# Low halves last in each pair of k tiles, the norm vector in a load of its own, the state-space parameter work behind the first weight chunk

## The chip, the cores and the metric

One core of a Trainium2 chip. The metric is the device time of one execution in us; before the change three runs gave 888.95, 889.18 and 889.61 us, median 889.18.

## The reference

A decoder trunk of two layers and a final norm on 256 tokens of 2048 channels, in float32. Cut to what matters here:

```python
# even layer: state-space mixer and spatial gating side by side
h = rmsnorm(x, norm_g); proj = h @ w_in
xa, ga, zb, gb = split(proj)
ya = gelu(s5_mixer(xa, ...)); ya = ya * sigmoid(ya @ w_glu + b_glu) * silu(ga)
u, v = split(gelu(zb)); v = layernorm(v)
yb = u * (causal(w_sp) mixed over 128 positions of v + b_sp) * silu(gb)
x = x + concat([ya, yb]) @ w_out
# odd layer: differential attention, 8 heads of two maps
q, k, v, g = split(rmsnorm(x, norm_g) @ w_in); q, k = partial_rope(q), partial_rope(k)
a = softmax(q1 @ k1.T) - lam * softmax(q2 @ k2.T)        # causal
o = rmsnorm(a @ v, subln_g) * (1 - lambda_init) * silu(g)
x = x + o @ w_out
return rmsnorm(x)
```

`s5_mixer` first works out its parameters from `lam`, `log_dt`, `B` and `C` (exponentials, sines, products of 64 states), then runs the recurrence.

## The kernel before, in words

All large products are made of **chunks** of the weights: `stream` lists 140 chunks of 1 MB, each 512 input rows (4 k tiles of 128) by 512 output columns. Chunks 0 to 7 are v, 8 to 15 xa, 16 to 23 u, 24 to 31 gb, 32 to 39 ga, 40 to 47 and 52 to 59 the first output projection (eo, ep) with the gate's weights between, 60 to 123 layer 1 (for each of four pairs of heads q, k, v, g, four chunks each), 124 to 139 the last output projection od. `fetch` (L139) loads chunks on SyncE's queue three ahead, `split` (L156) divides each into two halves b0 and b1 of two k tiles, and makes of each half two tiles of 32-bit reduced format: `wh`, the weight rounded, a copy on ScalarE (`act`, L82), and `wl`, the exact rest, a subtraction on VectorE (`sub`, L61). There are three buffers each for `wh` and `wl`, so a new half can be made when TensorE has done with one three halves back, or with any that has come free. Activations are divided likewise (`hh` and `hl` in layer 0, `oh` and `ol` ahead of od). A product takes three matmuls for each weight tile: hi·wh, hi·wl, lo·wh; `gemm_t` (L201, 512 columns a matmul, 24 a chunk) puts tokens on the partitions and `gemm_c` (L213, 256 columns, 48 a chunk) channels. c17_1 means half b1 of chunk 17, and wh17_1 its rounded tile.

Beside this runs side work: the parameters of the state-space mixer (`ssm_params` L359, `e_tables`, `ssm_consts`), its recurrence, and attention. These are Python generators in the queue `side`; `run_side(n)` takes n steps of them at a place in the source. `run_side(5)` stands ahead of the loop over v, `run_side(2)` behind each chunk of v. A scheduler then orders the instructions of TensorE, VectorE, ScalarE and GpSimd by readiness and priority (the halves of weights at a high one), so that the order on an engine isn't that of the source. SyncE's queue keeps the source's order. Each engine works its instructions through in the built order.

The parameters arrive as one packed tensor `pkt` of 82 KB, the first load of all (L259); its first 16 columns `g0` are the norm's weights, which `h_split` needs for the first `hh` and `hl`. The parameter work begins with an exponential of a part of `pkt` (tiles e_x, e_n, e_r, e_p on VectorE). Later its results go over ScalarE into `bbr` and `cA` (from the products m1fc, m2fc, m1fa, m2fa, m1ab, m2ab) and by 64 small matmuls into `pk0`; `pbt` are transposes of `bbr`, `U2` copies of the mixer's input, `vscr` a sum of squares for the layer norm of v, `vt` that norm's result, `ut` the evacuation of u.

In layer 1 each head h of a pair p has this chain: `sc{p}{h}` scores on TensorE, softmax, `aT{p}{h}` transposes, `ah`/`al`, `o{p}{h}` (nine matmuls), a norm (two sums of squares on ScalarE, twelve operations `rq_` and two scalings on VectorE), a product with the gate, `oT{p}{h}` transposes, `oh`/`ol`. The output projection takes its chunks in the order n = 0 and 1 with k = 0, 1, 2, then (0, 3) and (1, 3), that is c130 and c131: k tiles 12 to 15 are the last pair's output, and half b1 (tiles 14 and 15) is its second head's. od0 and od1 hold both banks of the PSUM pool for these products until then.

Of the kernel before, what the change touches and what calls it, by code (L numbers as in the profile page):

```python
# [17 lines left out]
T = 256  # L18
# [11 lines left out]
def hybrid_trunk_kernel(ctx: ExitStack, tc: tile.TileContext, xT, xtok, w_in0, w_glu, w_out0,  # L30
# [53 lines left out]
    def rsqrt_mean(name, ss, n, eps, post=None):  # L84
        """(ss / n + eps) ** -0.5: an integer first guess, a cubic step and a Newton step."""
# [32 lines left out]
    # ---------------------------------------------------------------- weight stream  # L118
# [20 lines left out]
    def fetch(upto):  # L139
        while pos["f"] <= min(upto, len(stream) - 1):  # L140
# [5 lines left out]
            for a in range(0, 4, step):  # L146
                if i < 4:
                    xs = slice(4 * i + a, 4 * i + a + step)
                    SP.dma_start(out=xt[:, xs, :], in_=xT[:, xs, :])
                SP.dma_start(out=t[:, a:a + step], in_=src[:, a:a + step])  # L150
# [5 lines left out]
    def split(upto, before=None):  # L156
        """hi = the weight rounded to float32r, lo = the exact rest."""
# [43 lines left out]
    def gemm_t(ps, acts, ktiles, first, last):  # L201
        ws = next_chunk()
        for a, k in enumerate(ktiles):
            hi, lo = acts(k)
            wh, wl = ws[a]
            for t in range(2):
                s = slice(t * 128, (t + 1) * 128)
                PE.matmul(ps[:, t, :], hi[:, s], wh, start=first and a == 0, stop=False)  # L208
                PE.matmul(ps[:, t, :], hi[:, s], wl, start=False, stop=False)  # L209
                PE.matmul(ps[:, t, :], lo[:, s], wh, start=False,  # L210
                          stop=last and a == len(ktiles) - 1)

    def gemm_c(ps, acts, ktiles, first, last):  # L213
        ws = next_chunk()
        for a, k in enumerate(ktiles):
            hi, lo = acts(k)
            wh, wl = ws[a]
            for c in range(4):
                s = slice(c * 128, (c + 1) * 128)
                fin = last and a == len(ktiles) - 1  # L220
                PE.matmul(ps[:, c, :], wh[:, s], hi, start=first and a == 0 and c % 2 == 0, stop=False,  # L221
                          skip_group_check=True)
                PE.matmul(ps[:, c, :], wh[:, s], lo, start=False, stop=False, skip_group_check=True)  # L223
                PE.matmul(ps[:, c, :], wl[:, s], hi, start=False, stop=fin, skip_group_check=True)  # L224
# [13 lines left out]
    # ---------------------------------------------------------------- start: x^T, norm  # L238
# [20 lines left out]
    SP.dma_start(out=pkt, in_=pk)  # L259
# [10 lines left out]
    g0 = pkt[:, 0:16]  # L270
# [854 lines left out]
```

## Time and profile before

| | |
|---|---|
| median of three runs | 889.18 us (888.95 to 889.61) |
| span of the profiled execution | 887.3 us |
| TensorE busy | 871.7 us, 98% |
| VectorE busy | 666.3 us, 75% |
| ScalarE busy | 448.8 us, 51% |
| GpSimd busy | 38.3 us, 4% |
| loaded and stored | 160.24 MB, mean 181 GB/s |

The profile is of one execution; its span runs from the first to the last instruction, and no other time of that execution is recorded. A share of busy time is an average over stages of different kinds, so the waits of TensorE stage by stage say more than the shares.

### The profile page before, as it was taken

The page shows a single profiled execution, that of the slowest core. Times are in us where ns is not written, and L with a number is a line of the kernel's source. Part 1 is how long each engine was busy: PE and PEld are TensorE (multiplying, and loading weights), DVE is VectorE, ACT ScalarE, POOL GpSimd, SP SyncE. Part 2 cuts the span into 40 slices and gives each one's busy share as a digit, 9 for nine tenths or more (in the row PEclk, how much of TensorE's full clock was granted, in tenths as well). Part 3 has the DMA queues.
Part 4 walks back from the last instruction along what each step waited for, and adds up shares of the span by engine and source line. Part 5 has one row for each costly group of instructions (what it writes and reads, how often), then busy time and mean ns, then how long its engine had stood idle before and what let it go on. Part 6 is the DMA issues. An engine that isn't in the chain of part 4 may idle for free.

```text
span 887.3 us, 14016 instructions
## 1 busy us (share of the span) xinstructions
PE 871.7 (98%) x5598; PEld 778.4 (88%) x5598; DVE 666.3 (75%) x1219; ACT 448.8 (51%) x623; POOL 38.3 (4%) x47
## 2 busy tenths in 40 slices
PE   9999999999999999999999999999999999999995
PEld 7799978788999789889988999889988998888895
DVE  8999869999988866567866677666767577665773
ACT  6563862455334645565345543554346544554551
POOL 7110000000000100000000000000000000000000
PEclk9999999999999999999999999999999999999998
DMA  8965452234534655455554545554454455555542
GB/s 306 379 243 191 143 190 96 96 120 166 190 114 141 259 185 176 170 195 202 180 182 160 188 145 190 191 190 152 181 190 171 165 188 196 183 189 190 178 155 96
DMA packets 25985, 160.24 MB, mean 181 GB/s; under 512 B 2880, under 2 KB 4160, under 8 KB 7744
## 3 DMA queue, kind: packets, MB, share of 16 engines
q1 hardware_dynamic: 25344, 156.20, 49.2%
q0 software_dynamic: 576, 3.15, 1.0%
q8 instruction: 44, 0.72, 0.3%
q14 instruction: 21, 0.17, 0.1%
HBM read 157.24 MB, written 2.10 MB: 180 GB/s over the span
## 4 chain that ended last, share of the span: by engine, by line
PE 90%; DVE 7%; ACT 1%; issue 1%; DMA 0%; DVEq 0%; ACTq 0%
PE v L209 5%; PE v L210 5%; PE v L208 5%; PE k L224 3%; PE q L221 3%; PE k L223 3%; PE k L221 3%; PE q L224 3%; PE q L223 3%; PE g L210 3%; PE g L209 3%; PE g L208 3%; PE od L209 2%; PE od L208 2%; PE od L210 2%; PE ga L221 2%
## 5 line engine op out<-in xcount | busy, mean ns | idle before, releaser
L82 ACT ACTIVATE wh<-wr 128x1024 fp32r<-128x1024 f32 (+1 forms) x276 | 288.7, 1047 | 356.0 <-PE v L210 64.0
L61 DVE TENSOR_TENSOR wl<-wr,wh 128x1024 fp32r<-128x1024 f32 (+1 forms) x276 | 331.8, 1205 | 142.2 <-ACT wh L82 141.4
L224 PE MATMUL k<-h2h,wl 128*128 128x256 f32 x256 | 72.8, 284 | 0.0
L221 PE MATMUL q<-h2h,wh 128*128 128x256 f32 x256 | 72.7, 284 | 0.0
L223 PE MATMUL q<-h2l,wh 128*128 128x256 f32 x256 | 72.7, 284 | 0.0
L224 PE MATMUL q<-h2h,wl 128*128 128x256 f32 x256 | 72.6, 284 | 0.0
L221 PE MATMUL k<-h2h,wh 128*128 128x256 f32 x256 | 72.4, 283 | 0.0
L223 PE MATMUL k<-h2l,wh 128*128 128x256 f32 x256 | 72.4, 283 | 0.0
L209 PE MATMUL v<-wl,h2h 128*128 128x512 f32 x128 | 50.8, 397 | 0.0
L209 PE MATMUL g<-wl,h2h 128*128 128x512 f32 x128 | 50.3, 393 | 0.0
L210 PE MATMUL g<-wh,h2l 128*128 128x512 f32 x128 | 50.1, 391 | 0.0
L210 PE MATMUL v<-wh,h2l 128*128 128x512 f32 x128 | 50.0, 390 | 0.0
L208 PE MATMUL v<-wh,h2h 128*128 128x512 f32 x128 | 50.0, 390 | 0.0
L208 PE MATMUL g<-wh,h2h 128*128 128x512 f32 x128 | 49.9, 390 | 0.0
L224 PEld LDWEIGHTS k<-h2h,wl 128*128 128x128 f32 x256 | 49.1, 192 | 0.1
L221 PEld LDWEIGHTS q<-h2h,wh 128*128 128x128 f32 x256 | 49.1, 192 | 0.2
L221 PEld LDWEIGHTS k<-h2h,wh 128*128 128x128 f32 x256 | 49.1, 192 | 0.0
L223 PEld LDWEIGHTS k<-h2l,wh 128*128 128x128 f32 x256 | 49.1, 192 | 0.0
L223 PEld LDWEIGHTS q<-h2l,wh 128*128 128x128 f32 x256 | 49.1, 192 | 0.0
L224 PEld LDWEIGHTS q<-h2h,wl 128*128 128x128 f32 x256 | 49.1, 192 | 0.0
L209 PE MATMUL od<-wl,oh 128*128 128x512 f32 x96 | 37.6, 392 | 0.0
L208 PE MATMUL od<-wh,oh 128*128 128x512 f32 x96 | 37.5, 391 | 0.0
(331 smaller groups left out, 2182.8 us busy)
## 6 DMA issues: line engine op xcount, KB each, us to landing
wr<-in_w_in_dram SPq DMA_DIRECT2D x100, 1024.0 KB, 4.8
wr<-in_w_out_dram SPq DMA_DIRECT2D x32, 1024.0 KB, 4.8
wr<-in_w_glu_dram SPq DMA_DIRECT2D x4, 1024.0 KB, 4.7
wr<-in_w_in_dram SPq DMA_DIRECT2D x8, 256.0 KB, 4.5
wr<-in_w_in_dram SPq DMA_DIRECT2D x4, 512.0 KB, 7.9
xk<-in_xtok_dram SPq DMA_DIRECT2D x2, 1024.0 KB, 10.9
xr<-in_xtok_dram POOLq DMA_DIRECT2D x2, 1024.0 KB, 7.6
out_dram<-x SPq DMA_DIRECT2D x6, 256.0 KB, 2.6
```

Source lines behind the costliest of these rows:

```text
L61: (eng or V).tensor_tensor(out=o, in0=a, in1=b, op=op)
L82: A.activation(out=o, in_=i, func=f, **kw)
L208: PE.matmul(ps[:, t, :], hi[:, s], wh, start=first and a == 0, stop=False)
L209: PE.matmul(ps[:, t, :], hi[:, s], wl, start=False, stop=False)
L210: PE.matmul(ps[:, t, :], lo[:, s], wh, start=False, stop=last and a == len(ktiles) - 1)
L221: PE.matmul(ps[:, c, :], wh[:, s], hi, start=first and a == 0 and c % 2 == 0, stop=False, skip_group_check=True)
L223: PE.matmul(ps[:, c, :], wh[:, s], lo, start=False, stop=False, skip_group_check=True)
L224: PE.matmul(ps[:, c, :], wl[:, s], hi, start=False, stop=fin, skip_group_check=True)
```

## The change

Three edits. **The loads:** `g0` becomes a tile of its own, loaded first (8 KB), and the whole `pkt` is loaded behind the second k tile's piece of chunk 0, sixth instead of first on SyncE's queue. **The matmuls:** in `gemm_t` and `gemm_c` all matmuls with the high half of two k tiles come first (hi·wh, lo·wh), then those with the low half (hi·wl); for chunk 0 this goes tile by tile. Their number is the same. **The side work:** `run_side(5)` ahead of the loop over v goes, and 7 steps instead of 2 are taken behind chunk 0. Comments that the diff removes are left out.

```diff
@@ fetch
             for a in range(0, 4, step):
+                if i == 0 and a == 2:
+                    SP.dma_start(out=pkt, in_=pk)
@@ gemm_t
+        i = pos["i"]
         ws = next_chunk()
-        for a, k in enumerate(ktiles):
-            hi, lo = acts(k)
-            wh, wl = ws[a]
-            for t in range(2):
-                s = slice(t * 128, (t + 1) * 128)
-                PE.matmul(ps[:, t, :], hi[:, s], wh, start=first and a == 0, stop=False)
-                PE.matmul(ps[:, t, :], hi[:, s], wl, start=False, stop=False)
-                PE.matmul(ps[:, t, :], lo[:, s], wh, start=False,
-                          stop=last and a == len(ktiles) - 1)
+        step = 1 if i == 0 else 2
+        for a0 in range(0, len(ktiles), step):
+            pair = range(a0, a0 + step)
+            for a in pair:
+                hi, lo = acts(ktiles[a])
+                for t in range(2):
+                    s = slice(t * 128, (t + 1) * 128)
+                    PE.matmul(ps[:, t, :], hi[:, s], ws[a][0], start=first and a == 0, stop=False)
+                    PE.matmul(ps[:, t, :], lo[:, s], ws[a][0], start=False, stop=False)
+            for a in pair:
+                hi, lo = acts(ktiles[a])
+                for t in range(2):
+                    s = slice(t * 128, (t + 1) * 128)
+                    PE.matmul(ps[:, t, :], hi[:, s], ws[a][1], start=False, stop=last and a == len(ktiles) - 1)
@@ gemm_c (likewise, always in pairs: 16 matmuls with wh, then 8 with wl)
...
@@ start
-    SP.dma_start(out=pkt, in_=pk)
+    g0 = const.tile([128, 16], F32, name="g0")
+    SP.dma_start(out=g0, in_=pk[:, 0:16])
...
-    g0 = pkt[:, 0:16]
@@ layer 0: v
-    run_side(5)
...
-            run_side(2)
+            run_side(7 if n == 0 and k == 0 else 2)
```

With this the scheduler's order changes in many places, also far from the edits. Three of them follow, in the order in which the engine gets its instructions; a name's last number tells buffers apart.

VectorE at the start, before (e_x to e_p are the exponential; hl0 and wl0_0 the low parts that the first matmuls need):

```order
L76 TENSOR_SCALAR e_x_215<-pkt_81 128x32
L61 TENSOR_TENSOR lprod_4116<-pkt_81 128x2
L74 TENSOR_SCALAR e_n_217<-e_x_215 128x32
L74 TENSOR_SCALAR e_n_217<-e_n_217 128x32 x2
L79 SCALAR_TENSOR_TENSOR e_r_221<-e_n_217,e_x_215 128x32
L79 SCALAR_TENSOR_TENSOR hl0_154<-xt_82,pkt_81,hh0_152 128x256
L79 SCALAR_TENSOR_TENSOR e_r_221<-e_n_217,e_r_221 128x32
L74 TENSOR_SCALAR e_p_224<-e_r_221 128x32
L74 TENSOR_SCALAR e_n1_233<-e_n_217 128x32
L79 SCALAR_TENSOR_TENSOR e_p_224<-e_p_224,e_r_221 128x32
L61 TENSOR_TENSOR wl0_0_157<-wr0_89,wh0_0_156 128x512
```

and now:

```order
L79 SCALAR_TENSOR_TENSOR hl0_156<-xt_82,g0_88,hh0_154 128x256
L61 TENSOR_TENSOR wl0_0_159<-wr0_90,wh0_0_158 128x512
L79 SCALAR_TENSOR_TENSOR hl0_156<-xt_82,g0_88,hh0_154 128x256
L76 TENSOR_SCALAR e_x_262<-pkt_81 128x32
L61 TENSOR_TENSOR lprod_4118<-pkt_81 128x2
L61 TENSOR_TENSOR wl0_0_159<-wr0_90,wh0_0_158 128x512
L74 TENSOR_SCALAR e_n_264<-e_x_262 128x32
```

The first hl0 and wl0_0 stand ahead of the exponential, and e_x now stands between the low halves of the first two k tiles.

ScalarE around chunks 16 and 17, where u begins, before:

```order
L82 ACTIVATE bbr1_648<-m2fc_659 64x32x16 x2
L82 ACTIVATE wh16_0_1653<-wr16_1535 128x1024
L82 ACTIVATE bbr0_646<-m1fa_702 64x32x16 x2
L82 ACTIVATE bbr1_648<-m2fa_703 64x32x16 x2
L82 ACTIVATE vscr0_934,vss_933<-vt_212,mu_930 128x1024
L82 ACTIVATE vscr1_961,vss_960<-vt_212,mu_957 128x1024
L82 ACTIVATE wh16_1_1657<-wr16_1535 128x1024
L82 ACTIVATE cA_650<-m1ab_714 64x32x16 x2
L82 ACTIVATE wh17_0_2021<-wr17_1593 128x1024
L82 ACTIVATE cA_650<-m2ab_715 64x32x16 x2
L82 ACTIVATE U2_208<-xs0_1267 32x512 x8
L82 ACTIVATE wh17_1_2025<-wr17_1593 128x1024
```

and now:

```order
L82 ACTIVATE wh16_1_1659<-wr16_1537 128x1024
L82 ACTIVATE wh17_0_2023<-wr17_1595 128x1024
L82 ACTIVATE bbr1_650<-m2fc_661 64x32x16 x2
L82 ACTIVATE bbr0_648<-m1fa_704 64x32x16 x2
L82 ACTIVATE bbr1_650<-m2fa_705 64x32x16 x2
L82 ACTIVATE vscr0_936,vss_935<-vt_214,mu_932 128x1024
L82 ACTIVATE vscr1_963,vss_962<-vt_214,mu_959 128x1024
L82 ACTIVATE cA_652<-m1ab_716 64x32x16 x2
L82 ACTIVATE cA_652<-m2ab_717 64x32x16 x2
L82 ACTIVATE U2_210<-xs0_1269 32x512 x8
L82 ACTIVATE vt_214<-vt_214,vnb_954,vrs_943 128x1024
L82 ACTIVATE wh17_1_2027<-wr17_1595 128x1024
```

wh17_0 has moved ahead of m2fc, m1fa, m2fa, vscr and the first cA, so that these, the second cA, U2 and one vt now lie between wh17_0 and wh17_1, where only the second cA and U2 lay.

TensorE in the last output projection, around the transposes of the last head (oT31), before (the rest of c128_1, all of c129 and the start of c130_0 stand between the nine matmuls of o31 and these rows):

```order
L208 MATMUL od0_7850<-wh130_0_8024,oh8_6842 128x512
L209 MATMUL od0_7850<-wl130_0_8025,oh8_6842 128x512
L210 MATMUL od0_7850<-wh130_0_8024,ol8_6843 128x512
L924 MATMUL oT31_7838<-ident_132,o231_7834 128x128 x4
L208 MATMUL od1_7953<-wh131_0_8058,oh8_6842 128x512
L209 MATMUL od1_7953<-wl131_0_8059,oh8_6842 128x512
```

and now, from the last three of o31's nine matmuls on (the first two stand ahead of c131_0's four low-half matmuls, the other seven behind them):

```order
L920 MATMUL o31_7804<-v_hi_4158,ah31_7800 128x256
L920 MATMUL o31_7804<-los_4159,ah31_7800 128x256
L920 MATMUL o31_7804<-v_hi_4158,al31_7801 128x256
L935 MATMUL oT31_7840<-ident_134,o231_7836 128x128 x4
L214 MATMUL od0_7852<-wh130_1_8030,oh8_6844 128x512
L214 MATMUL od1_7955<-wh131_1_8064,oh8_6844 128x512
L215 MATMUL od0_7852<-wh130_1_8030,ol8_6845 128x512
```

o31 has moved behind the high-half matmuls of c131_0, and oT31 follows its last matmul directly; the first product behind oT31 is c130_1, where it was c131_0.

## Rows read from the trace of the kernel before

**Rows 1.** The page: busy time, share of the span and instructions of TensorE (PE), its weight loads (PEld), VectorE (DVE), ScalarE (ACT), GpSimd (POOL).
```profile
PE 871.7 (98%) x5598; PEld 778.4 (88%) x5598; DVE 666.3 (75%) x1219; ACT 448.8 (51%) x623; POOL 38.3 (4%) x47
```

**Rows 2.** The windows view, one stretch of the span, within layer 1. Columns: the stretch in us and its length, busy us (and instructions) of PE, PEld, DVE, ACT, POOL, the granted clock of TensorE (1.00 is the upper of its two levels), the share of the DMA engines, GB/s.
```profile
420.00:780.00 360.00, 360.00 (x2340) 329.60 (x2340) 250.78 (x382) 175.81 (x250) 6.75 (x8) 1.00 0.51 179
```

**Rows 3.** The waits of TensorE: tile and line that waited, the engine and tile waited for, us in total, times, the longest.
```profile
PE v L209 <- DVE wl L61: 1.6, 2, 0.8
PE gb L208 <- ACT ut L82: 1.4, 1, 1.4
...
PE u L209 <- DVE wl L61: 0.8, 1, 0.8
PE pbt L521 <- ACT bT L82: 0.8, 1, 0.8
PE u L208 <- ACT ut L82: 0.5, 1, 0.5
PE eo L209 <- DVE wl L61: 0.4, 1, 0.4
```

**Rows 4.** The timeline of the start. Columns: start us, duration us, engine, line, operation, out<-in, shapes, and in brackets the idle time ahead of it and what ended it. hh and hl are the two parts of the activations; L208, L209 and L210 are the matmuls hi·wh, hi·wl and lo·wh.
```profile
3.53 0.51 ACT L82 ACTIVATE hh<-xt,pkt 128x256 fp32r<-128x256 f32 x1 [1.22 <-DMA xt<-in_xT_dram]
...
5.53 0.51 DVE L79 SCALAR_TENSOR_TENSOR hl<-xt,pkt,hh 128x256 fp32r<-128x256 f32 x1
...
5.85 0.80 PE L208 MATMUL v<-wh,hh 128*128 128x512 f32 x1
...
6.74 0.68 DVE L61 TENSOR_TENSOR wl<-wr,wh 128x512 fp32r<-128x512 f32 x1
...
7.47 0.80 PE L209 MATMUL v<-wl,hh 128*128 128x512 f32 x1 [0.82 <-DVE wl L61]
...
9.77 0.63 PE L208 MATMUL v<-wh,hh 128*128 128x512 f32 x1
...
10.20 0.53 PE L209 MATMUL v<-wl,hh 128*128 128x512 f32 x1
...
10.80 0.40 PE L208 MATMUL v<-wh,hh 128*128 128x512 f32 x1
...
11.03 0.39 PE L209 MATMUL v<-wl,hh 128*128 128x512 f32 x1
...
11.26 0.39 PE L210 MATMUL v<-wh,hl 128*128 128x512 f32 x1
```

**Rows 5.** The timeline of ScalarE from 92 to 116 us, where parameter work of the state-space mixer stands between the weight halves (same columns).
```profile
92.72 1.26 ACT L82 ACTIVATE bbr<-m2fc 64x512 f32<-64x512 f32 x2
...
96.93 1.27 ACT L82 ACTIVATE bbr<-m2fa 64x512 f32<-64x512 f32 x2
98.23 1.15 ACT L82 ACTIVATE vscr<-vt,mu 128x1024 f32<-128x1024 f32 x1
...
101.60 1.25 ACT L82 ACTIVATE cA<-m1ab 64x512 f32<-64x512 f32 x2
103.12 1.06 ACT L82 ACTIVATE wh<-wr 128x1024 fp32r<-128x1024 f32 x1 [0.26 <-PE xa L223]
...
105.36 5.30 ACT L82 ACTIVATE U<-xs 32x512 f32<-32x512 f32 x8
...
111.65 1.23 ACT L82 ACTIVATE vt<-vt,vnb,vrs 128x1024 f32<-128x1024 f32 x1
```

**Rows 6.** The timeline of TensorE about 97 to 99 us: the first and the last row of pk0's 64 small matmuls.
```profile
97.04 0.22 PE L506 MATMUL pk<-cN,bbr 128*32 128x32 f32 x1
...
99.03 0.23 PE L506 MATMUL pk<-cN,bbr 128*32 128x32 f32 x2
```

**Rows 7.** The timeline from 812 to 829 us, where the last head's attention ends: the last matmul of o31 (o), of its norm on VectorE the ninth of twelve operations, the scaling (o<-o,ro, two operations), the gate, the transposes oT31 (oT) and their two parts oh and ol. In between a low half of a weight (wl) on VectorE, behind the eighth of them, and two matmuls of the output projection (od) on TensorE.
```profile
814.97 0.28 PE L909 MATMUL o<-v_hi,al 128*128 128x256 f32 x1
...
817.77 1.23 DVE L61 TENSOR_TENSOR wl<-wr,wh 128x1024 fp32r<-128x1024 f32 x1
...
818.92 0.15 DVE L61 TENSOR_TENSOR rq_z<-ro 128x2 f32<-128x2 f32 x1
...
819.70 0.88 DVE L79 SCALAR_TENSOR_TENSOR o<-o,ro,l1c 128x256 f32<-128x256 f32 x2
...
821.64 0.68 DVE L61 TENSOR_TENSOR o<-o,gate 128x512 f32<-128x512 f32 x1
821.69 0.39 PE L210 MATMUL od<-wh,ol 128*128 128x512 f32 x1
...
824.41 0.39 PE L210 MATMUL od<-wh,ol 128*128 128x512 f32 x1
...
824.65 0.60 PE L924 MATMUL oT<-ident,o 128*128 128x128 f32 x4
...
825.81 0.58 ACT L82 ACTIVATE oh<-oT 128x512 fp32r<-128x512 f32 x1
...
827.08 0.68 DVE L61 TENSOR_TENSOR ol<-oT,oh 128x512 fp32r<-128x512 f32 x1
```

**Rows 8.** The timeline of TensorE at the program's end (two matmuls of 256 columns, the second its last), and the windows view of the last 6 us (columns as in rows 2).
```profile
873.83 0.28 PE L1016 MATMUL od3b<-hlast,oh 128*128 128x256 f32 x1
...
878.03 0.28 PE L1018 MATMUL od3b<-hlast,ol 128*128 128x256 f32 x1
...
881.00:887.30 6.30, 0.00 (x0) 0.00 (x0) 1.80 (x6) 0.72 (x1) 0.00 (x0) 0.50 0.44 166
```

More of the change, by code (lines that the diff above doesn't have):

```diff
@@ L213, in gemm_c @@
     def gemm_c(ps, acts, ktiles, first, last):
         ws = next_chunk()
[L215 to L224, printed above, removed]
+        cs = [(c, slice(c * 128, (c + 1) * 128)) for c in range(4)]
@@ new lines, in gemm_c @@
+        for a0 in range(0, len(ktiles), 2):
+            for a in (a0, a0 + 1):
+                hi, lo = acts(ktiles[a])
+                for c, s in cs:
+                    PE.matmul(ps[:, c, :], ws[a][0][:, s], hi, start=first and a == 0 and c % 2 == 0, stop=False,
+                              skip_group_check=True)
+                    PE.matmul(ps[:, c, :], ws[a][0][:, s], lo, start=False, stop=False, skip_group_check=True)
+            for a in (a0, a0 + 1):
+                hi, lo = acts(ktiles[a])
+                for c, s in cs:
+                    PE.matmul(ps[:, c, :], ws[a][1][:, s], hi, start=False, stop=last and a == len(ktiles) - 1,
+                              skip_group_check=True)
```

## Prediction

> **What bounds the kernel now.** I read the page first: TensorE is busy 98% of the span, VectorE 75, ScalarE 51 [rows 1]. So the time is TensorE's instructions plus TensorE's holes, and the views to read next are those that show holes. The windows say where to look: in 420 to 780 us TensorE is busy all of 360.00 us [rows 2], so nothing waits there. The list of TensorE's waits names the holes one by one: two of 0.8 us in v for the low half of a weight, 1.4 at gb for ut, 0.8 in u for a low half, 0.8 at pbt for bT, 0.5 in u for ut, 0.4 in eo for a low half [rows 3]. They add up to 5.5 us of 887.3. All sit in layer 0; layer 1, where two thirds of the time lies, has none. So this kernel offers a reordering little to win and, with TensorE full, much to lose: any new hole is paid in full.
>
> The profiled span is 887.3 us, the median of the runs 889.18, 1.9 us more, lying around the span. I work out differences inside the span and add them to 889.18. A measurement here can tell 0.2%, 1.8 us, from no change.
>
> **The matmuls themselves: 0.** The diff only permutes them. Every matmul loads its own weights before and after (as many weight loads as matmuls [rows 1]), and the three forms follow each other at the same 0.23 us once the clock is up [rows 4]. So putting the low-half matmuls last is free, and what counts is only who arrives when.
>
> **Start: -0.9.** The first matmul, on the high half, starts at 5.85, the next one at 7.47, because it needs the low half that VectorE began at 6.74 only, behind e_x, e_r and e_p [rows 4]. After the change hl·wh stands second; hl was written at 5.53 with its inputs there at 4.1, so nothing is waited for. The hole is 1.62 less one cold spacing of 0.43 (9.77 to 10.20), so 1.19 us. But these matmuls run at half speed until 10.20: if the clock rises at the same moment, 1.19 us hold 2.8 more cold matmuls, worth 2.8 x 0.23 = 0.64 later. If it rises as much earlier as the work does, all 1.19 is won. I take 0.9 between them; bounds 0 (e_x must now wait for the parameter load, which is issued behind four pieces, and VectorE's next low half queues behind e_x) and -1.2. The small first load only brings g0, and hh starts at 3.53 anyway when its piece of x arrives [rows 4], so it is worth nothing by itself.
>
> **Low halves later needed: -0.8 and -0.4.** The second v wait and the eo wait [rows 3] are for a low half wanted one matmul behind the first high one. Now eight matmuls, 1.8 us, come first, which is more than either wait. Bounds 0 and the full 1.2 together; I take the full.
>
> **The parameter work behind chunk 0: +4.2.** This is the first new hole. ScalarE's queue now has wh17_0 ahead of both m2fc operations, both a-sets, vscr, both cA, U2 and one vt, and wh17_1 behind all of them (the ScalarE order above). wh17_0 needs a buffer that TensorE frees with the last high-half matmul of c15_1; call that moment T. From T ScalarE needs 1.06 (wh) + 1.26 + 2 x 1.27 (bbr: m2fc, m1fa, m2fa, whose operations are of one shape) + 2 x 1.15 (vscr) + 2 x 1.25 (cA) + 5.30 (U) + 1.23 (vt) + 1.06 (wh17_1) = 17.2 us [rows 5]. TensorE has for that time: eight low-half matmuls at 0.12 (1.0), pk0 from 97.04 to 99.03 (2.1 [rows 6]) and pbt (1.0), and 36 matmuls of c16 and c17_0 at 0.227 (8.2), together 12.2. So 5.0 us are idle, in three pieces: pk0 for m2fc (1.06 + 1.26 - 0.96 = 1.4), pbt00, which needs pk0's bank read out, and c17_1 for the rest. Before, u lost 0.8 at this place [rows 3]. Net +4.2. Bounds: 0 if the operations of rows 5 find their turn as early as before, +6 if vscr's readouts and gaps between operations lengthen the queue by a tenth.
>
> **Waits that vanish behind it: -2.7.** TensorE comes about 2 us late to pbt's second half and both ut hand-overs (0.8, 0.5, 1.4 [rows 3]), and on ScalarE bT and ut now stand at most one operation further forward. I take all three as gone; bounds -2.7 and 0.
>
> By here the change stands at -0.9 - 0.8 - 0.4 + 4.2 - 2.7 = -0.6, about nothing.
>
> **The end of attention: +6.3.** This is the term that decides. In the output projection, half b1 of c130 and c131 needs the last head's output: o31, its norm, oT31, then oh and ol. Before, TensorE has the rest of c128_1, all of c129 and c130_0 between o31 and oT31: 42 matmuls, 9.7 us from 814.97 to 824.65, and the chain fits inside [rows 7]. After the change the scores of a pair are mostly put behind g, all of attention slides some 20 us, and the order above has nothing between o31 and oT31, with c130_1 right behind. The chain costs, from the start of the last o31 matmul: 2.80 to the end of eight of the twelve norm operations (814.97 to 817.77, two readouts on ScalarE ahead of them); 0.78 for four more (818.92 to 819.70); 0.80 for both o2; 0.68 for the gate. That is 5.06; the two low halves that stood within it are now ahead or behind. Then oT31 0.60, oh 0.58, ol 0.68 [rows 7], some 0.3 of hand-overs: 7.2. TensorE's own work in this time is the last o31 (0.1), four oT31 (0.4) and two high-half matmuls (0.45): 6.3 idle. Bounds 4.1 (the 5.06 alone less that work) and 7.2 (all of it).
>
> **The clock: +2.1.** At the end of the profile TensorE stops at 878.3, and from 881.0 on the granted clock is 0.50, its 1.2 GHz level [rows 8]: it fell within 2.7 us of the stop. The hole above holds 4.9 us without a matmul. So I expect the clock to fall in it, and c130_1 to start at the 0.43 spacing. At the start matmuls of v ran at that spacing from 5.85 to 10.20; the same 4.35 us here do the work of 2.3, so 2.1 are lost. Bounds: 0 (the clock stays), and 4.2 if the slow stretch lasts twice as long. The Trainium skill, "TensorE: Matmul & The Clock Gate", section "Part 1: The HAM clock gate (the "warmup" mystery)", says that the count of slow matmuls after a start varies from run to run of one kernel; no run so far shows that, and by it this term would be no constant, and the sum 895 to 897 from run to run.
>
> **Sum:** 889.18 - 0.6 + 6.3 + 2.1 = 896.98, so 897.0 us.
>
> **The rivals.**
> *The clock holds.* Four transposes and two matmuls interrupt the hole; if they keep the clock at its upper level only 6.3 is paid: 889.18 - 0.6 + 6.3 = 894.9. For it: the hole of 1.4 us before gb [rows 3] left the granted clock at 1.00. Against it: the fall at the end. Chance 0.28.
> *The spacing shrinks, so faster.* Place: all 84 chunks of 24 matmuls of 512 columns and 52 of 48 of 256, with od3 some 4700 matmuls. Putting two matmuls on the high half before one on the low half changes which operand follows which, and a spacing smaller by d ns gives 4.7 us per ns of d; from 1.3 ns on it wipes out 6.0 of the 7.8 and the time is within 0.2%, from 2.1 ns on it is faster: with 2.3 ns, 1% of 227, 897.0 - 10.8 = 886.2. For it: the spacing of 0.227 (12 steps from 821.69 to 824.41 [rows 7]) and 0.120 (35 steps from 873.83 to 878.03 [rows 8]) is above what 2.4 GHz would make of 512 and 256 columns, 0.213 and 0.107. Against it: two forms that share hi follow each other exactly as two that don't [rows 4]. The Trainium skill, "TensorE: Matmul & The Clock Gate", section "Wait — 56ns, not 53.3ns?", gives 215.7 ns for back-to-back matmuls of 512 columns; the trace differs, 227, and by the page's spacing the room for this rival would be 11 ns. Chance 0.08, and 0.03 that a milder form leaves the time the same.
> *The late attention collides everywhere.* Scores of all four pairs move behind g, into the next pair's q, where VectorE also works on q's rotation. If three boundaries each cost one low half, 1.2 us, and c132 another 0.5, the time is 897.0 + 4.1 = 901.1. Against: at each there are 4 to 10 us of matmuls between a score and its use. Chance 0.08.
>
> **How the numbers follow.** Forecast 897.0: 0.53. Its own range by the bounds that I think live (start, queue and clock each 1 us off): 895.5 to 899. The clock rival reaches down to 894.9, less 2.5 if the chain is at its lower bound or the queue fits better: 892.3. These two have 0.81, and 892 to 899.5 leaves little of them out. Slower by over 0.2% (above 891.0): 0.53 + 0.28 + 0.08 = 0.89. The same: 0.03. Faster (below 887.4): 0.08.
>
> **What would show it.** Right: the waits of TensorE list oT <- VectorE (the gated o2) with 4 to 5 us in one piece near 825, then od <- ScalarE or VectorE for oh and ol; the granted clock is 0.50 for some us right behind; matmuls of od at 0.43 spacing; u or pk waits of 1 to 3 us near 100 to 116, no v <- wl wait at 5.85 and 42, no gb <- ut. Wrong: no wait at oT above 1 us, matmuls of layer 1 closer than 0.227 and 0.120 (the second), a hole of 5 us with the clock at 1.00 throughout (the first), waits of about a microsecond at each q of layer 1 (the last), or in layer 0 a sum that differs from -0.6 by more than 2.

## The result, and the profile after

The changed kernel takes 901.1 us (median of four runs, 900.06 to 901.86) against 889.07 before: ratio 1.0131, 95% interval 1.0117 to 1.0145, slower by 12.0 us where 7.8 were forecast, and outside the range. The profiled execution took 900.49 us, 0.6 below the median; its span is 898.8 (before 887.3).

The busy line of the page after, which answers to [rows 1]:

```profile
PE 874.3 (97%) x5598; PEld 780.2 (87%) x5598; DVE 668.0 (74%) x1219; ACT 451.1 (50%) x623; POOL 37.8 (4%) x47
```

The work is the same. TensorE is busy 2.6 us longer, which goes with matmuls at the lower clock; the rest is holes. The waits of TensorE after (columns as in [rows 3]):

```profile
PE oT L935 <- DVE o L61: 5.1, 1, 5.1
PE u L214 <- DVE rq_i L74: 1.9, 1, 1.9
PE v L220 <- DVE wl L61: 1.6, 1, 1.6
PE pk L518 <- ACT bbr L82: 1.4, 1, 1.4
PE pbt L533 <- DVE intra L61: 1.2, 1, 1.2
...
PE od L214 <- ACT oh L82: 0.7, 1, 0.7
PE gb L214 <- ACT ut L82: 0.6, 1, 0.6
PE u L214 <- ACT ut L82: 0.5, 1, 0.5
```

Five waits of over a microsecond, where before only gb had one (psw's 1.1 at the very start, left out, is there in both). Those of oT, pk and pbt were forecast; v's was not, and u's was put at another place, at c17_1 instead of u's first matmul. A list of waits misses what a slow clock costs, so the table below uses another measure: for each matmul the time to the next one's start, less the median for its shape (227 ns for 512 columns, 120 for 256, 109 for 128, 25 for 32, the same before and after), added up by stretch of the span. Small negative sums come from pairs of unlike shapes; the differences between rows are what counts. E1 to E14 are the experiments below.

| us lost in | 0–20 | 20–80 | 80–120 | 120–180 | 180–420 | 420–820 | from 820 | sum |
|---|---|---|---|---|---|---|---|---|
| before | 5.5 | 1.1 | 1.1 | 3.5 | -3.5 | 1.3 | 0.1 | 8.9 |
| after | 4.6 | 2.0 | 6.2 | 1.9 | -3.4 | 0.1 | 8.7 | 20.2 |
| E1 old order from layer 1 on | 5.0 | 3.1 | 6.1 | 2.0 | -3.4 | 1.3 | 0.1 | 14.0 |
| E2 new order alone | 5.1 | 0.6 | 4.7 | 1.6 | -3.7 | 0.1 | 9.6 | 17.8 |
| E3 loads and side work | 5.8 | 1.6 | 6.1 | 3.4 | -4.5 | 1.4 | 0.1 | 13.9 |
| E4 loads, chunk 0 | 5.1 | 1.6 | 6.2 | 3.0 | -4.8 | 1.3 | 0.1 | 12.5 |
| E5 after, hole filled | 5.0 | 1.9 | 6.1 | 2.0 | -3.4 | 0.2 | 4.9 | 16.6 |
| E6 after, early clearings | 4.0 | 0.0 | 6.1 | 2.0 | -3.4 | 0.1 | 9.8 | 18.5 |
| E7 chunk 0 alone | 5.8 | 1.0 | 1.1 | 3.7 | -3.7 | 1.2 | 0.1 | 9.2 |
| E8 loads alone | 5.6 | 1.4 | 6.4 | 2.8 | -4.8 | 1.3 | 0.1 | 12.8 |
| E9 after, m2fc first | 4.3 | 1.9 | 6.9 | 1.6 | -3.4 | 0.2 | 8.8 | 20.2 |
| E10 three chunks | 5.6 | 0.5 | 0.4 | 2.4 | -3.1 | 1.2 | 0.1 | 7.1 |
| E11 three chunks, early clearings | 8.9 | 0.0 | 0.4 | 3.8 | -4.5 | 1.3 | 0.1 | 9.8 |
| E12 more VectorE work | 7.0 | 0.2 | 7.5 | 1.9 | -4.5 | 1.4 | 0.1 | 13.6 |
| E13 as E2, two low halves back | 4.4 | 0.6 | 2.4 | 1.8 | -3.0 | 0.1 | 9.5 | 15.8 |
| E14 after, two low halves back | 5.1 | 1.9 | 6.2 | 1.6 | -3.4 | 0.2 | 9.8 | 21.4 |

After less before, from the unrounded sums: -0.9, +0.9, +5.1, -1.5, +0.1, -1.1, +8.7; together 11.2 of the span's 11.5.

**The end of attention.** The timeline after from o31's last matmul on (columns as in [rows 4]; answers to [rows 7]):

```profile
829.76 0.28 PE L920 MATMUL o<-v_hi,al 128*128 128x256 f32 x1
...
833.40 0.88 DVE L79 SCALAR_TENSOR_TENSOR o<-o,ro,l1c 128x256 f32<-128x256 f32 x2
834.31 0.69 DVE L61 TENSOR_TENSOR o<-o,gate 128x512 f32<-128x512 f32 x1
835.15 1.09 PE L935 MATMUL oT<-ident,o 128*128 128x128 f32 x4 [5.11 <-DVE o L61]
836.27 0.60 ACT L82 ACTIVATE oh<-oT 128x512 fp32r<-128x512 f32 x1 [5.36 <-PE oT L935]
...
836.92 1.22 PE L214 MATMUL od<-wh,oh 128*128 128x512 f32 x2 [0.69 <-ACT oh L82]
837.94 0.63 PE L215 MATMUL od<-wh,ol 128*128 128x512 f32 x1
838.37 0.63 PE L214 MATMUL od<-wh,oh 128*128 128x512 f32 x1
...
```

The same chain as in [rows 7], now with nothing beside it: 5.11 us without a matmul, then 0.69 for oh. The four transposes take 1.09 instead of 0.60, and od steps by 0.43 until 840.07. The windows view there (columns as in [rows 2]) tells why:

```profile
830.00:833.00 3.00, 0.04 (x1) 0.00 (x0) 2.24 (x12) 0.84 (x4) 0.00 (x0) 1.00 0.61 254
833.00:836.00 3.00, 0.85 (x4) 0.71 (x4) 1.83 (x5) 0.00 (x0) 0.00 (x0) 0.55 0.00 0
836.00:838.00 2.00, 1.31 (x5) 0.85 (x4) 0.69 (x1) 0.60 (x1) 0.00 (x0) 0.50 0.00 0
838.00:840.00 2.00, 2.00 (x6) 1.59 (x5) 0.00 (x0) 0.00 (x0) 0.00 (x0) 0.50 0.00 0
840.00:842.00 2.00, 2.00 (x10) 1.58 (x9) 0.13 (x1) 1.06 (x1) 0.00 (x0) 0.97 0.00 0
```

The granted clock falls within the hole and is back soon after 840. Attention did slide, as forecast: the last scores of the four pairs come 20 to 22 us later by the span, the last matmul of o31 14.8 us (829.76 instead of 814.97).

**The parameter work.** The timeline after of VectorE, ScalarE and TensorE from 97 to 109 us, where the mixer's parameters are used:

```profile
97.53 0.68 DVE L61 TENSOR_TENSOR m2fc<-m2fc 128x512 f32<-128x512 f32 x1
99.56 1.06 ACT L82 ACTIVATE wh<-wr 128x1024 fp32r<-128x1024 f32 x1 [2.12 <-PE xa L231]
100.53 1.25 ACT L82 ACTIVATE bbr<-m2fc 64x512 f32<-64x512 f32 x2
101.83 0.22 PE L518 MATMUL pk<-cN,bbr 128*32 128x32 f32 x1 [1.35 <-ACT bbr L82]
103.10 1.29 DVE L61 TENSOR_TENSOR m2ab<-bct,ab 128x512 f32<-128x512 f32 x2
104.31 1.38 DVE L61 TENSOR_TENSOR intra<-pk,intra 32x512 f32<-32x512 f32 x2
105.83 0.63 PE L533 MATMUL pbt<-ident,bbr 128*128 128x128 f32 x4 [1.20 <-DVE intra L61]
107.10 1.22 DVE L61 TENSOR_TENSOR xs<-xa,rbc 128x1024 f32<-128x1024 f32 x1
108.38 0.50 PE L214 MATMUL u<-wh,hh 128*128 128x512 f32 x1 [1.92 <-DVE rq_i L74]
...
110.46 0.63 PE L215 MATMUL u<-wh,hl 128*128 128x512 f32 x1
```

Three holes in a row: pk0 for m2fc behind wh17_0 on ScalarE, pbt for intra, u for xs (108.32; the row names rq_i, the operation behind it). VectorE is busy for 21.8 of the 22 us from 86 to 108. From 110 to 113 the granted clock is 0.50, though no single hole is longer than 1.9 us.

### The profile page after: what moved, and what is told of

Same layout as the page of the kernel before. It is cut to its first block, busy times and chain, and to the rows that moved or that the text cites. A ratio compares the mean times of both kernels' runs of the same rounds, so it can differ in the third digit from the quotient of the medians.

```text
span 898.8 us, 14093 instructions
## 1 busy us (share of the span) xinstructions
PE 874.3 (97%) x5598; PEld 780.2 (87%) x5598; DVE 668.0 (74%) x1219; ACT 451.1 (50%) x623; POOL 37.8 (4%) x47
## 4 chain that ended last, share of the span: by engine, by line
PE 93%; DVE 3%; DMA 1%; ACT 1%; SPq 1%; issue 0%; DVEq 0%; ACTq 0%
PE v L214 4%; PE v L220 4%; PE v L215 4%; PE q L235 3%; PE k L235 3%; PE k L231 3%; PE k L229 3%; PE q L229 3%; PE q L231 3%; PE g L214 3%; PE g L215 3%; PE g L220 3%; PE od L214 3%; PE od L215 2%; PE od L220 2%; PE y L618 2%
## 5 line engine op out<-in xcount | busy, mean ns | idle before, releaser
L231 PE MATMUL k<-h2l,wh 128*128 128x256 f32 x256 | 63.5, 284 | 0.0
L231 PE MATMUL q<-h2l,wh 128*128 128x256 f32 x256 | 63.5, 284 | 0.0
L229 PE MATMUL q<-h2h,wh 128*128 128x256 f32 x256 | 63.3, 283 | 0.0
L215 PE MATMUL od<-wh,ol 128*128 128x512 f32 x96 | 38.4, 400 | 0.0
L235 PE MATMUL q<-h2h,wl 128*128 128x256 f32 x256 | 37.8, 285 | 0.0
L235 PE MATMUL k<-h2h,wl 128*128 128x256 f32 x256 | 35.9, 283 | 0.0
L220 PE MATMUL v<-wl,h2h 128*128 128x512 f32 x128 | 34.7, 393 | 0.0
L220 PE MATMUL g<-wl,h2h 128*128 128x512 f32 x128 | 34.2, 389 | 0.0
L235 PEld LDWEIGHTS q<-h2h,wl 128*128 128x128 f32 x256 | 33.6, 192 | 0.0
L235 PEld LDWEIGHTS k<-h2h,wl 128*128 128x128 f32 x256 | 33.0, 192 | 0.0
```

The costliest lines, as they stand in the source:

```text
L215: PE.matmul(ps[:, t, :], lo[:, s], ws[a][0], start=False, stop=False)
L220: PE.matmul(ps[:, t, :], hi[:, s], ws[a][1], start=False, stop=last and a == len(ktiles) - 1)
L229: PE.matmul(ps[:, c, :], ws[a][0][:, s], hi, start=first and a == 0 and c % 2 == 0, stop=False, skip_group_check=True)
L231: PE.matmul(ps[:, c, :], ws[a][0][:, s], lo, start=False, stop=False, skip_group_check=True)
L235: PE.matmul(ps[:, c, :], ws[a][1][:, s], hi, start=False, stop=last and a == len(ktiles) - 1, skip_group_check=True)
```

## The experiments

**E1: which part makes the hole at the end?** The changed kernel, with the old loops of gemm_t and gemm_c for layer 1 and od:

```diff
+    def gemm_t1(...)   # and gemm_c1: as before the change
...
-            gemm_t(ps, h2_acts, ...)
+            gemm_t1(ps, h2_acts, ...)
```

> The changed kernel with the old order of the three matmuls from layer 1 on (layer 0, loads and side work as changed). Theory: the hole of 5.1 us before oT31 and the low clock behind it come from the new order of layer 1's matmuls alone, which cost 8.7 us there and won 1.1 elsewhere in layer 1; so about 901.1 - 8.7 + 1.1 = 893.5 us, no wait at oT31, clock 1.00 from 780 us on, layer 0 as in the changed kernel. Rival: attention is late because the side work starts later in layer 0; then the hole stays and the time is 900 to 902.

894.0 us, ratio to before 1.0047 (1.0034 to 1.0059). No oT wait is left, and from 820 on 0.1 us is lost. The new order of the matmuls from layer 1 on makes that hole; layer 1 and od were not tried apart. It also wins 1.1 us in 420 to 820: all kernels with the new order there lose 0.1 or 0.2, all with the old 1.2 to 1.4.

**E2: the matmuls alone.** The new gemm_t and gemm_c in the kernel before; loads and side work as before.

> The kernel before with the new order of the matmuls in all layers; loads and side work as before. Theory: the holes at 100 to 108 us (5.1 us net) come from the new order too, and the low-half wait in chunk 6 only from the later side work. Then start -0.9, chunk 6 -0.8, 100 to 120 us +5, the waits behind it -1.5, layer 1 -1.1, tail +8.7: about 898.5 us. Rival: the holes at 100 us come from the later side work; then about 893.5 us.

897.96 us, 1.0094 (1.0079 to 1.011). The end is there in full (oT 5.1), but the holes of 80 to 120 as well: 4.7. So the order of the matmuls suffices for them, too.

**E3: loads and side work, old order.** The load edits, and run_side(5) moved behind chunk 0.

> The kernel before with the two loads and the later side work, the matmuls in the old order. Theory: the start wins 0.5 to 0.9 (the low half comes earlier), chunk 6 loses about 1.8 (VectorE's small operations are caught longer by GpSimd's two memsets), the rest stays: 889.5 to 890.5 us, no hole at 100 us, none at oT31. Rival (the side work makes the holes at 100 us): 894.

893.6 us, 1.0045 (1.0032 to 1.0057). The expectation failed; the rival's time came, 80 to 120 loses 6.1 without any new matmul order, but E4 and E8 show that its reason, the side work, isn't needed for it.

**E4: chunk 0.** The load edits, and in chunk 0 alone lo·wh ahead of hi·wl; run_side as before.

> The kernel before with the two loads, and the low half last in chunk 0 only. Theory: the wait at the start goes and little else moves: 888.2 us (-0.9). Rival: the later parameter load delays VectorE's chain and chunk 6 gives it back: 889 to 890.

893.06 us, 1.0042 (1.0029 to 1.0054). Both expectations missed by 3 us or more: with run_side back in its place 80 to 120 loses as much, 6.2. What E3 and E4 share is the loads. From here the theory is: VectorE, 75% busy over the span, is nearly full from 5 to 108 us (99.4 of 103 us before), and what it loses early comes out where its chain is used.

**E8: the loads alone.**

```diff
+                if i == 0 and a == 2:
+                    SP.dma_start(out=pkt, in_=pk)
...
-    SP.dma_start(out=pkt, in_=pk)
+    SP.dma_start(out=g0, in_=pk[:, 0:16])
```

> The kernel before with the two load edits alone: g0 first in a tile of its own, the parameters sixth on the queue. Matmuls and side work as before. Theory (VectorE is nearly full from 5 to 100 us, so that the 3.5 us for which it idles at the start without the parameters come back as holes where their chain is used): 892.8, bounds 891.8 and 893.8, 100 to 120 us loses 5 to 6 instead of 1.6, intra starts at 102 to 104 instead of 99.58. Rival (the load is harmless, the side work and the matmul order made the holes): 889.2, 100 to 120 as before.

893.4 us, 1.0049 (1.0036 to 1.0062): the load alone costs 4 us, and with the later side work it costs no more (E3, 893.6). The windows view of the first 10 us, two lines of the kernel before, then two of E8 (columns as in [rows 2]):

```profile
0.00:5.00 5.00, 3.87 (x18) 3.87 (x19) 2.40 (x5) 1.99 (x3) 4.26 (x10) 1.00 0.48 134
5.00:10.00 5.00, 4.10 (x11) 2.81 (x11) 4.90 (x20) 3.92 (x8) 5.00 (x7) 1.00 0.97 320
...
0.00:5.00 5.00, 3.87 (x18) 3.87 (x19) 0.65 (x2) 1.99 (x3) 4.23 (x9) 1.00 0.46 124
5.00:10.00 5.00, 4.95 (x17) 2.95 (x16) 3.21 (x9) 3.39 (x7) 2.75 (x5) 1.00 0.95 300
```

VectorE (the third busy figure) is busy for 3.86 us of these 10; before it was 7.30. Of these some 1.7 are e_x, the first operation of the parameter work, standing still beside a clearing by GpSimd (in the changed kernel it takes 0.18; more on this at E6). The timeline of the kernel before:

```profile
2.70 1.88 DVE L76 TENSOR_SCALAR e_x<-pkt 128x32 f32<-128x32 f32 x1 [1.62 <-DMA pkt<-in_pk_dram]
```

intra starts at 103.0 instead of 99.6. Up to there VectorE is busy for 94.0 us, before for 93.9, so the 3.4 us are more idle time. The work is not quite the same: 38 low halves of weights stand ahead of intra, 37 before, and e_x takes 1.7 less. 80 to 120 loses 5.3 us more, but only a part of it at the holes of the changed kernel: pbt and u wait 0.8 and 1.3 us, and then c17_1 for its two halves (before, 0.8 for the low one):

```profile
PE u L211 <- DVE wl L61: 2.1, 1, 2.1
PE u L210 <- ACT wh L82: 1.3, 1, 1.3
```

**E7: chunk 0 with the early load.** The kernel before, with lo·wh ahead of hi·wl in chunk 0.

> The kernel before with one edit: in chunk 0 of gemm_t lo x wh stands before hi x wl. The parameter load stays first, the side work where it was. Theory (the later parameter load made the +3.8 of the kernel with chunk 0 reordered and both loads): the start wins 0.4 to 0.9 and all else stays, 888.4, bounds 888.0 and 888.9; 100 to 120 loses 1.6 as before. Rival (the small reordering itself shifts the built order and makes the holes): 892 to 893.

889.36 us, 1.0003 (0.9994 to 1.0012). No holes at 100, so a small reordering does not bring them. But the start's gain isn't there either (5.8): with the parameters there early, e_x and its kin stand ahead of wl0_0 again, and TensorE waits for that one matmul later. The changed kernel's order in chunk 0 is another, with four matmuls ahead of the first low half instead of two; E2 and E13 have it with the early load, and lose 5.1 and 4.4 by 20 us.

**E12: more work for VectorE.** The kernel before with three products whose results nobody uses:

```diff
+    dum = t4("dum", [128, 4, T])
+    for z in range(3):
+        mul(dum, xt[:, 4 * z:4 * z + 4], xt[:, 4 * z:4 * z + 4])
```

> The kernel before with three products of 128x1024 (1.22 us each, 3.7 in all) added on VectorE in the first 20 us, their result unused; matmul order, loads and side work as before. Theory (VectorE is full up to 108 us, so that anything it loses early comes out as holes where the parameter work is used): 892.6, bounds 891.5 and 893.5, 100 to 120 us loses 4.5 to 6 instead of 1.6, intra starts at 102 to 103.5 instead of 99.58. Rival (VectorE has room to catch up): 889.3.

893.37 us, 1.0052 (1.0037 to 1.0067). 3.8 us of VectorE work between 9 and 21 us cost 4.0, with two of the waits of the changed kernel; the waits of TensorE in E12:

```profile
PE pbt L521 <- DVE intra L61: 2.2, 1, 2.2
PE u L208 <- DVE rq_i L74: 1.5, 1, 1.5
```

intra starts at 104.5, later than expected, xs at 107.3. Neither loads nor matmuls were touched, but the built order moved here too: 39 low halves stand ahead of intra instead of 37. Of what makes intra 5.0 us late 3.8 are the products and 2.3 the two low halves; VectorE is idle for 4.8 us ahead of intra, before for 5.7, so it caught up by 0.9 and no more.

**E9: is it ScalarE's queue, as predicted?** The changed kernel, wh17_0 made to wait for m2fc:

```diff
+                        if i == 17 and b == 0:
+                            act(h[:, 0, 0:1], bbr[1][:, 0, 1, 0:1], AF.Copy)
                         act(h[:, e], w[:, e], AF.Copy)
```

> The changed kernel with wh17_0 made to wait for m2fc: one column of it is first written from bbr, so that on ScalarE bbr<-m2fc (2 x 0.63 us) stands ahead of wh17_0, as in the kernel before; on VectorE wl17_0 and intra each move one place back, little else moves. Theory (VectorE, busy without a gap from 86 to 108 us, sets when u begins): the 1.4 us wait of pk0 goes, the wait of pbt for intra grows by as much or more, xs stays at 107 and u at 108.4: 901.0, bounds 900.3 and 901.6. Rival (ScalarE's queue sets it, as the prediction had it): u begins 1.4 to 2.2 us earlier, 899.2.

900.92 us, 1.013 (1.0116 to 1.0144), as the changed kernel. pk0 starts without a wait, at 100.05 behind the last xa matmul, and then pbt waits for intra; two of E9's waits:

```profile
PE pbt L535 <- DVE intra L61: 2.9, 1, 2.9
PE u L216 <- DVE rq_i L74: 1.3, 1, 1.3
```

intra stays at 104.3, and the wait moves from pk to pbt; u begins at 107.73 instead of 108.38, and a longer stretch at the lower clock (from 106 to 113 instead of 110 to 113) takes that back. So the place of wh17_0 on ScalarE, on which the forecast was built, is worth nothing by itself.

**E6: GpSimd's clearings.** One wait was still without a cause: 1.6 us at c6 for wl6_0. The timeline after of VectorE and GpSimd from 34 to 39 us:

```profile
34.62 0.19 DVE L61 TENSOR_TENSOR e_p<-e_p,e_i 128x32 f32<-128x32 f32 x1
34.74 1.81 POOL L481 MEMSET cA<- 128x2048 f32 x1 [13.57 <-ACT xsq L82]
34.74 1.84 DVE L74 TENSOR_SCALAR ph_y<-ph 128x32 f32<-128x32 f32 x1
...
36.77 1.81 POOL L482 MEMSET cN<- 128x2048 f32 x1 [0.23 <-ACT xsq L82]
36.84 1.78 DVE L74 TENSOR_SCALAR ph_s<-ph_z 128x32 f32<-128x32 f32 x1
```

An operation that takes 0.18 elsewhere takes 1.84 and 1.78, each time until a clearing of 1.81 us ends. E6 lets xk live in two other slots, so that the clearings of cA and cN needn't wait for it:

```diff
-    xk = [t8(9 + t, f"xk{t}", [128, D]) for t in range(2)]
+    xk = [t8(13 - t, f"xk{t}", [128, D]) for t in range(2)]
...
-            act(scr, xk[t], AF.Square, ...)
+            act(xk[t], xk[t], AF.Square, ...)
```

> The changed kernel with xk in two other slots and its squares written in place, so that GpSimd's two clearings of cA and cN, 1.81 us each, no longer stand at 34 to 39 us but come early; nothing else moves. Theory (VectorE's small operations stand still beside these clearings, and so the low half for c6 comes 1.6 us late, and the parameter chain with it): no v <- wl wait over 0.4 near 44, intra up to 2 us earlier than 104.31, the 100 to 120 stretch loses 4 to 5 instead of 5.9, time 898.0, bounds 897 and 899.5. Rival (the clearings only hide other waiting): 901, the c6 wait stays at 1.2 to 1.6.

898.91 us against 901.1. The c6 wait is gone (20 to 80: 2.0 to 0.0), all TENSOR_SCALAR and COPY operations at 30 to 42 us take 0.16 to 0.19. But the 4 to 5 us expected for 100 to 120 didn't come, the block from 80 on still loses 6.1: intra comes 2.6 us earlier, and so does TensorE.

**E5: the clock.** The changed kernel, with seven products of ones on the last head's squares between o31 and oT31, their result unused:

```diff
             ro = rsqrt_mean("ro", so, 256, RMS_EPS, post=1.0 - LAMBDA_INIT)
+            # for the last head, ahead of this line:
+            PE.matmul(fill[:, 0:256], ones, scr[:, 1], ...)   # x 7
```

> The changed kernel with seven matmuls of ones on the last head's scaled squares put between o31 and oT31, their result unused; nothing else moves. Theory (of the 8.7 us lost at the end of attention some 2.3 are the clock at its lower level behind the hole): the clock stays at 1.00, the oT31 transposes take 0.60 instead of 1.09 and od follows at 0.227 instead of 0.43, so 898.8, bounds 898.3 and 899.3, while o, gate, oh and ol come when they came. Rival (the slow matmuls there are not the clock's doing, or the dummies come too early to hold it): 901.1 as the changed kernel, spacing 0.43 again.

898.59 us. (In the table the dummies count as work, 1.7 us, so its 4.9 is not what is lost there.) The windows view of E5 there:

```profile
833.00:836.00 3.00, 2.12 (x12) 1.49 (x10) 2.10 (x7) 0.00 (x0) 0.00 (x0) 1.00 0.00 0
836.00:838.00 2.00, 1.31 (x6) 0.73 (x5) 0.69 (x1) 0.60 (x1) 0.00 (x0) 1.00 0.00 0
838.00:840.00 2.00, 2.00 (x11) 1.62 (x10) 0.00 (x0) 0.55 (x1) 0.00 (x0) 1.00 0.03 8
```

The clock stays at 1.00 with the same chain, 5.39 us from o31's last matmul to oT31 in both, and the time falls by 2.5 us: that is what the fall of the clock costs by the medians. By the spans of the two profiled executions it is 1.8.

**E10: the new order only where a low half was late.** The kernel before; c6, c17 and c41 with their low-half matmuls last in each pair of k tiles:

```diff
+        pairs = i in (6, 17, 41)
...
+            if pairs:
+                todo.sort(key=lambda z: z[2] == 2)   # hi x wl behind hi x wh and lo x wh
```

> The kernel before with the new matmul order in three chunks alone, those whose second matmul waited for a low half: c6, c17 and c41. Loads and side work as before. The holes there are 1.0, 1.0 and 0.5 us beyond the spacing. Theory (VectorE is full up to 108 us, so what TensorE wins at c6 it waits for near 100 to 116; what it wins at c17 and c41 it keeps): 887.6, bounds 886.9 and 888.5; 100 to 120 loses no less than 1.6 though the c17 wait is gone. Rival 1 (all three are kept): 886.6. Rival 2 (nothing is kept): 889.

887.53 us, 0.998 (0.9972 to 0.9989), 1.8 us faster than the kernel before. The waits at c6, c17 and c41 are gone; of the 2.5 us of these holes 1.8 were won. That c6's gain would be given back near 100 did not come true (80 to 120: 0.4); beyond the spacing 0.4 us are lost at xa near 59 us and 0.5 at c18, whose low half is still wanted second.

**E11: E10 with early clearings.** The edits of E10 and E6.

> The kernel with the new order in c6, c17 and c41, and xk in two other slots so that GpSimd's clearings of cA and cN come early instead of at 34 to 39 us. The order of VectorE and TensorE stays. Theory (VectorE stands still for 1.75 us beside these clearings and is full up to 108 us): it comes to the parameter work up to 1.7 us earlier and the part that the three chunks alone give back is kept: 886.7, bounds 886.0 and 887.5, faster than before by more than 0.2%. Rival (the clearings cost nothing on the path): as the three chunks alone.

890.63 us, 1.0013 (1.0004 to 1.0022): the expectation failed, E10 is 3 us better. The timeline of E11 from 4.5 to 11 us:

```profile
4.82 1.83 POOL L476 MEMSET cA<- 128x2048 f32 x1
4.94 3.52 DVE L74 TENSOR_SCALAR e_n<-e_n 128x32 f32<-128x32 f32 x2
...
6.59 1.84 POOL L477 MEMSET cN<- 128x2048 f32 x1
10.42 0.79 PE L218 MATMUL v<-wl,hh 128*128 128x512 f32 x1 [4.31 <-DVE wl L61]
```

The clearings now meet e_n, which takes 3.52 us for two operations (0.45 in E10), with wl0_0 behind it; TensorE waits 4.31 for wl0_0, and the granted clock falls to 0.50 from 8 us on. In E6 the parameters came later, and the clearings met e_x alone (1.27 us). This is the strongest sign that the clearings stop VectorE: they were moved, and the stop moved with them.

**E13 and E14: why the new order alone makes the holes.** In the built order of E2 and of the changed kernel 39 low halves stand ahead of intra on VectorE, 37 before: wl16_1 and wl17_0, 2.4 us, have moved ahead. (With the load alone, E8, one has.) E13 puts these two back in E2, E14 in the changed kernel:

```diff
+                        if (i, b) in ((16, 1), (17, 0)):
+                            mul(l[:, 0, 0:1], cst["intra"][:, 0, 0:1], cst["intra"][:, 0, 0:1])
                         sub(l[:, e], w[:, e], h[:, e].bitcast(F32))
```

> The kernel with the new matmul order alone, and on VectorE wl16_1 and wl17_0 made to wait for intra by a product of one column of intra written into them first, so that both stand behind xs as in the kernel before the change. Theory (with the new order these two low halves, 2.4 us, have moved ahead of intra, and that makes the holes near 100 us without any late load): xs up to 2.4 us earlier than 104.96, 80 to 120 us loses 2.3 instead of 4.7, time 895.6, bounds 894.5 and 896.6. Rival (the holes have another cause, the low halves are only then needed anyway): 898, or as much again in waits of u for a low half.

896.96 us (E2 897.96); 80 to 120 loses 2.4 instead of 4.7, as expected, xs starts at 103.5 instead of 105.0. The time misses by a little, its runs lying between 895.7 and 898.2: from 820 on nothing has changed.

> The changed kernel with the same edit: wl16_1 and wl17_0 wait for intra and stand behind xs. Theory: xs up to 2.4 us earlier than 107.10, 80 to 120 us loses 4 instead of 6.2, the rest being the late load, time 898.9, bounds 898.0 and 900.0. Rival: 901.

900.65 us, and 6.2 as before: the rival. The timeline of VectorE in E14 shows what holds it now:

```profile
102.32 1.29 DVE L61 TENSOR_TENSOR m1ab<-bct,ab 128x512 f32<-128x512 f32 x2 [2.38 <-ACT bbr L82]
...
106.03 1.39 DVE L61 TENSOR_TENSOR intra<-pk,intra 32x512 f32<-32x512 f32 x2
107.70 1.23 DVE L61 TENSOR_TENSOR xs<-xa,rbc 128x1024 f32<-128x1024 f32 x1
```

m1ab needs a buffer that ScalarE frees with bbr<-m2fc, which stands behind wh17_0; in the changed kernel wl17_0 filled that time. So two queues are late there side by side, ScalarE's by wh17_0 and VectorE's by two low halves. E9 takes away the first, E14 the second, and each time the other one holds. Both at once was not tried.

## Why the prediction was wrong, step by step

The terms of the start, the end and the clock came in size; those that failed are the low half at c6, the cause of the parameter work's holes, and the waits that were to vanish.

**Matmuls 0: right to within 1.1.** Spacings of 227 and 120 ns before and after. What I took for nothing to win in layer 1, because TensorE's window there reads 360.00 of 360.00 [rows 2], held small steps of up to 0.1 us, many of them where matmuls of attention stand between those of v and g, and they add up to 1.1 us less after the change; busy shares hide them because matmuls overlap. That they go with the new order E1 shows; why, no run tells.

**Start -0.9: right in size**, -0.9 in these two executions. By 20 us the five kernels with the changed start (after, E1, E5, E9, E14) lose 4.3 to 5.1, the two with the old one (before, E10) 5.5 and 5.6, so the gain lies between 0.4 and 1.3. hh starts at 3.48, 3.53 before, so the small load brings nothing by itself, as said. Nor is the later parameter load needed for the gain: E2 and E13 have it with the early one.

**Low halves later needed -0.8 and -0.4: the first failed.** At c6 the stretch of 20 to 80 loses 0.9 more instead of 0.8 less (2.0 more in E1, whose wait at c6 is 2.7 us). The step took eight matmuls, 1.8 us, as more than the wait, with the low half's time unchanged; but wl6_0 itself came later, held up by the clearings: they stopped VectorE's small operations for 1.84 and 1.78 us, before for 1.19 and 0.56. With the clearings moved (E6), or with the early load (E2, E10), the wait is won. The eo wait is gone, but its stretch is no shorter.

**Parameter work +4.2: the size nearly right (+5.1), by luck; the cause wrong.** The failed step is the sum on ScalarE's queue alone. The three holes are 4.5 us against 5.0; matmuls at the lower clock from 110 to 113 us, behind holes of under 2 us each, add some 1.5 that the step didn't have. pk0's 1.4 us came as written, but the third piece was not c17_1 for wh17_1, and with wh17_0 back in its place nothing is won (E9). Two things make VectorE's chain late, and I priced neither: the load moved from first to sixth place leaves it idle early (E8: 5.3 us lost at 80 to 120), and of a delay it makes up little (0.9 us in E12); and the new order puts two low halves ahead of intra (E2 3.6, of which E13 takes back 2.3). In the changed kernel intra is 4.7 us late; ahead of it VectorE is idle for 8.2 us instead of 5.7 and busy for 96.1 instead of 93.9, so a little over half of it is idle time and the rest more work, about the two low halves. The losses of TensorE do not add up so, 5.1, since more than half of E8's stand at c17_1, where the changed kernel doesn't wait. [rows 1] shows VectorE at 75%, an average over the program; I read only TensorE stage by stage, and the load I priced within a bound of the start.

**Waits that vanish -2.7: -1.5.** pbt's went, ut's at u stayed (0.5), gb's went from 1.4 to 0.6 only. The step took the full bound on each; what holds ut there no run tells.

**End of attention +6.3 and clock +2.1: right**, 8.7 against 8.4. The chain took 5.11 + 0.69, and E5 prices the clock at 2.5 (1.8 by the spans). What the Trainium skill says in "TensorE: Matmul & The Clock Gate", section "Part 1: The HAM clock gate (the "warmup" mystery)", on the varying count of slow matmuls is what the runs point to: behind the same wait of 5.1 us od runs slow for 3.2 us from its first start in the changed kernel, 5.7 in E2, E6 and E14, which have the same matmuls from layer 1 on, and E13's runs lie 2.4 us apart, those of the kernel before beside it 1.3.

**The rivals.** The clock did not hold. The spacing did not shrink. "Late attention collides everywhere" had 901.1, which is the time measured, by chance: none of its waits came, and layer 1 before the end won.

By terms, forecast and measured: start -0.9 and -0.9; c6 -0.8 and +0.9; block +4.2 and +5.1; vanishing waits -2.7 and -1.5; eo -0.4 and +0.1 in its stretch; layer 1 0 and -1.1; end 8.4 and 8.7. The 3.4 us missing lie at c6 (1.7), in the block (0.9) and behind it (1.2 at waits that stayed, 0.5 at eo, 0.3 at the end), less the 1.1 of layer 1. Up to 420 us the sum is +3.7 instead of -0.6, which is one of the signs that the prediction named for being wrong.

## What to carry to other kernels

Ask of the second engine what you ask of the first: is it full in this stretch, and from when to when? Where it is, an idle microsecond at the start, a transfer issued a little later, can be paid in full where its chain is used, 95 us on here (E8). And apply a reordering where a wait is (three chunks, 1.8 us won) rather than everywhere, since the built order far away moves with it.

## What the runs showed of the hardware

A clearing by GpSimd (128x2048, 1.81 us) stops VectorE's 128x32 TENSOR_SCALAR operations until it ends (1.84 and 1.78 us instead of 0.18), while a 128x1024 TENSOR_TENSOR (wl at 37.00) beside the second clearing (from 36.85) kept its 1.22 us in the kernel before. The sixteen traces hold 29 TENSOR_SCALAR operations that came up beside such a clearing with nothing held up ahead of them, and each ended 0.03 to 0.05 us behind the clearing; operations with two inputs in that place were not held, nor were four RECIPROCAL operations (0.34 us). The Trainium skill, "SBUF — State Buffer", section "Who interferes with whom", says that single-input operations of VectorE in a two-port mode and GpSimd exclude each other for a whole instruction, and that an operation with two inputs in SBUF isn't held up by one that only writes; these rows agree, though none shows the mode of an operation.

The granted clock fell to 0.50 behind one hole of 5.1 us and one of 4.3, and also at 110 us behind holes of 1.4, 1.2 and 1.9 us. In E8, with holes of 0.8 and 1.3 us at 104 to 106, it stayed at 1.00 up to 119; in E4, with 0.8 and 1.2 us there, it fell at 106. So the length of the holes alone does not tell.
